# Splitting two raw weight tiles of the first two summed pairs at the FFN entry: accumulating DMA in place of two subtractions

## The chip, the cores and the metric

The kernel runs on one core of a Trainium2 chip. The metric is the device time of one execution in microseconds (us), as a median over runs. The engines are TensorE (PE in the profile; its weight loads are the row PEld), VectorE (DVE), ScalarE (ACT), GpSimd (POOL) and SyncE (SP), whose queue issues most of the DMAs. An engine name with a q behind it (SPq) is the engine's queue.

## The reference, cut to what matters

The program is one step of a two-layer streaming encoder: a Mamba-2 mixer with a SwiGLU FFN (layer 0), then banded attention with a SwiGLU FFN (layer 1), for 1024 prompt rows and 64 new rows of another stream, in float32. The change lies in the first half of the FFN, the product with `w_in`, in both layers:

```python
def swiglu(u, w_in, w_out):
    g, up = jnp.split(u @ w_in, 2, axis=-1)
    return (jax.nn.silu(g) * up) @ w_out
```

The model width is 1024. The hidden width is 2816, that is 22 tiles of 128 columns of `g` and 22 of `up`.

## The kernel before, in words

**Split operands.** Each float32 operand is split into a high part, rounded to the type float32r, and a low part, the operand less its high part. A product is three matmuls into one PSUM bank: high by high, high by low, low by high. A weight tile of 128 x 1024 comes from memory into a `raw` tile. `Weights.part` (L327) splits it into an `hl` tile with room for both parts: ScalarE copies the high part (L340), then VectorE subtracts it from the raw tile (L341). For the ring `half` (128 x 512) GpSimd does the subtraction.

**A second way to split.** Some tiles carry the mark `acc`. For them ScalarE writes the high part (L334), then its negative into the place of the low part (L335); then GpSimd issues a DMA that reads the raw weights from memory again and adds them to what stands there (L336). What is left there is the low part. Neither VectorE nor a GpSimd subtraction is used, but the low part has landed only when the DMA has. Before the change the mark is set for `w_in` tiles of the first six hidden tiles (L1256), for four of them: 0, 1, 2 and 5.

**The order of the FFN.** `ffn_plan` lists the weights in the order of their use. The first six hidden tiles are computed plainly for the first half of the rows (`plain_pairs`: one tile of `g`, one of `up`, each by eight slices of 128). While this runs, the second half of the rows is still being normalised and split (`chain`, `op_build`; L1167 to L1200 on VectorE and ScalarE). From hidden tile 6 on, the tiles of `g` and `up` are not multiplied one by one: `run_pair` forms seven products of half-size blocks in the place of eight, a Strassen-like scheme. The last six pairs of this list are the tiles 0 to 5 again, for the second half of the rows.

**A pair.** `Weights.pair` prepares a pair from its two raw tiles `r0` (of `g`) and `r1` (of `up`). With blocks b11, b21 (halves of `r0`) and b12, b22 (halves of `r1`): GpSimd computes two differences (L290, L291) into the two tiles `ta`, `tb` of the ring `tt`; `b22` is split into `half`; `r0` is split into `hl`; VectorE finishes the sums (L308, L309); `ta` and `tb` are split into `hl`. The products use them in the order r0, ta, r0, ta, tb, tb, b22. The low part of `r0` is read by the third matmul of the first product.

**Tiles that set the pace.** There are two `raw` tiles, three `hl`, two `tt` and two `half`. A raw tile is loaded anew by SP's queue (L252) when all its readers are done. An `hl` tile comes free when the last product that reads it is through: for `r0` of a pair that is the third product. So `r0` of pair 7 can be split only when TensorE is past the third product of pair 6, `ta` and `tb` of pair 7 later still. For pair 6 the seven products are run for the first half of the rows, then for the second half.

**The order on each engine.** TensorE's instructions run in the order in which the program writes them; a planner with estimated costs (`st`) fits side work between them. On the other engines a scheduler orders the instructions by readiness and priority; the copies and subtractions of `part` for the first pairs have the highest priority (`W.pri = HIP`), the accumulating DMA has none of its own. Each engine works its list in order, so an instruction that waits holds up those behind it.

**Lines that matter.** PSUM evictions of the plain tiles: L1282 (ScalarE), L1286 (VectorE). Evictions of the products: L1321 to L1341. The matmuls of the products: L1309, L1310 (high part of the weights), L1311 (low part). Splits of the second half of the rows: L1179 (ScalarE), L1180 (VectorE).

Of the kernel before, what the change touches and what calls it, by code (L numbers as in the profile page):

```python
# [12 lines left out]
ALU = mybir.AluOpType  # L13
# [20 lines left out]
FT = 22  # L34
# [29 lines left out]
NB0 = 6  # L64
# [160 lines left out]
class Weights:  # L225
# [56 lines left out]
    def pair(self, it):  # L282
        r0, r1 = it["raw"]
        b11, b21, b12, b22 = r0[:, :512], r0[:, 512:], r1[:, :512], r1[:, 512:]
        if "T" not in it:
            if not self.tt.free(2):
                return False
            ta, tb = it["T"] = self.tt.get(), self.tt.get()
            g = self.nc.gpsimd.tensor_tensor
            g(ta[:, 512:], b22, b12, op=ALU.subtract)  # L290
            g(tb[:, :512], b12, b11, op=ALU.subtract)  # L291
            return True
        ta, tb = it["T"]
        if "b22" not in it and self.half.free():
            self.part(it, "b22", self.half, b22, self.nc.gpsimd)
            it["of"][1].put()
            return True
        if "r0" not in it:
            if not self.hl.free():
                return False  # L300
            self.part(it, "r0", self.hl, r0)
            self.ready.append(it)

            return False
        if "sums" not in it:
            v = self.nc.vector.tensor_tensor
            with self.tc.high_priority(self.pri):
                v(ta[:, :512], ta[:, 512:], b11, op=ALU.add)  # L308
                v(tb[:, 512:], b21, ta[:, :512], op=ALU.subtract)  # L309
            it["of"][0].put()  # L310
            it["sums"] = True
            return True
        for key, src in (("ta", ta), ("tb", tb)):
            if key not in it:
                if not self.hl.free():
                    return False
                self.part(it, key, self.hl, src)
                self.tt.put()
                return True
        if "b22" not in it:  # L320
            return False
        self.sq.pop(0)
        return True

    def part(self, it, key, ring, v, eng=None):
        if ring is not self.half:
            ring = self.hl if ring or self.hl.free() else self.hx  # L327
            self.used.append(ring)
        t, n = ring.get(), v.shape[1]
        h, lo = t[:, 0, :n], t[:, 1, :n]  # L330
        if it.get("acc"):

            with self.tc.high_priority(self.pri):
                self.nc.scalar.copy(h, v)  # L334
                self.nc.scalar.activation(lo, h, AF.Copy, scale=-1.0)  # L335
            self.nc.gpsimd.dma_start(lo, it["src"][0], accum_op=ALU.add)  # L336
            it[key] = h, lo
            return
        with self.tc.high_priority(self.pri):
            self.nc.scalar.copy(h, v)  # L340
            (eng or self.eng or self.nc.vector).tensor_tensor(lo, v, h, op=ALU.subtract)  # L341
        it[key] = h, lo
# [32 lines left out]
def hybrid_kernel(  # L375
# [33 lines left out]
    for _ in range(17):  # L409
# [14 lines left out]
    W = Weights(  # L424
        nc, Ring(wp, "raw", RAWB, [P, 1024]), Ring(wp, "hl", HLB, [P, 2, 1024], F32R),
        Ring(None, "half", 0, [P, 2, 512], F32R), Ring(None, "tt", 0, [P, 1024]),
    )
# [826 lines left out]
    def ffn_plan(layer):  # L1254
        w1, w2 = w_f1[layer], w_f2[layer]
        W.plan(*[dict(src=[w1[i]], acc=t_ < NACC or t_ == NB0 - 1) for t_ in range(NB0) for i in (t_, FT + t_)])  # L1256
        for t_ in [*range(NB0, FT), *range(NB0)]:
            W.plan(dict(src=[w1[t_], w1[FT + t_]]))
        for s in range(NSL):
            for m in range(KD):  # L1260
                for k0, nk in KCH:
                    W.plan(dict(src=[w2[m][:, k0 * P:(k0 + nk) * P]], n=nk * P))
# [274 lines left out]
    def start_ssd(ops, px, after, dn):  # L1537
# [10 lines left out]
        st.spawn(op_build(ops[1], dn))  # L1548

    ffn_plan(0)  # L1550
    rbp = pool(ctx, "rbp", side="right")
    rba = [rbp.tile([P, 384], F32, tag=f"rbf{s}", name="rbf") for s in range(NSL)]
# [14 lines left out]
    for mg in MGS[:2] + MGS[:1] + MGS[2:] + MGS:  # L1567
        W.plan(*[dict(src=[w_o[m]]) for m in mg])
    ffn_plan(1)
    done = done2  # L1570
    uo, part_o = {}, {}
# [485 lines left out]
```

## Time and profile before

| | |
|---|---|
| median of 3 runs | 2942.54 us (2942.36 to 2943.93) |
| profiled execution, own time | 2945.22 us |
| its span in the profile | 2943.5 us |
| granted TensorE clock, mean | 0.996 |
| ScalarE splits L340 `hl` from `raw`, 128 x 1024 | 1047 ns (median) |
| VectorE subtraction L341 `hl` from `raw`, 128 x 1024 | 1224 ns (median) |
| GpSimd subtraction L341 `half` from `raw`, 128 x 512 | 1294 ns (median) |

The profile is of one execution. A row of a timeline gives the start and the length in us, engine, line, operation, and output <- input by the program's names; a bracket behind it gives the idle time of that engine before it and what released it. Matmuls overlap each other, so the distance from start to start, about 0.11 us for 256 columns, says more than the length of one. The granted clock is the share of full speed that TensorE was given.

### The profile page before, as it was taken

The numbers are of one execution on the slowest core, as the hardware profiler recorded it, in microseconds if no ns is written. First come the engines' busy times: TensorE is split into PE (matmuls) and PEld (weight loads), VectorE is DVE, ScalarE is ACT, GpSimd is POOL, SyncE is SP. The second block draws the span as 40 slices with busy tenths as digits, with TensorE's granted clock in tenths as the row PEclk, the third lists the DMA queues.
The fourth block names the chain that finished last, engine by engine and source line by source line (L and its number), as shares of the span: only waits on it lengthen the run. The fifth ranks groups of instructions, "written<-read, shape, count | busy, mean of one in ns | idle before, by whom it ended". The sixth has DMA issues, their size and how long they took to land.

```text
span 2943.5 us, 56260 instructions
## 1 busy us (share of the span) xinstructions
PE 2904.2 (99%) x21562; PEld 2864.1 (97%) x21562; DVE 2026.4 (69%) x4452; ACT 1401.6 (48%) x2531; POOL 724.4 (25%) x884
## 2 busy tenths in 40 slices
PE   8999999999999999999999999999999999999999
PEld 8999999999999999999999899999999999999999
DVE  7988878885867555583567787778688555575544
ACT  6655546454543222353445665556664322244443
POOL 1333333331022434351111000000131434351111
PEclk9999999999999999999999999999999999999999
DMA  4423333335564222345665322223376222245654
GB/s 138 132 92 106 103 100 106 100 120 159 165 187 123 76 84 73 111 151 163 206 189 157 90 80 72 64 69 103 124 204 177 79 83 73 82 153 175 223 172 137
DMA packets 202846, 368.07 MB, mean 125 GB/s; under 512 B 20688, under 2 KB 149424, under 8 KB 202576
## 3 DMA queue, kind: packets, MB, share of 16 engines
q1 hardware_dynamic: 199920, 354.97, 38.5%
q0 software_dynamic: 2656, 9.51, 1.8%
q8 instruction: 169, 2.77, 0.4%
q14 instruction: 101, 0.83, 0.1%
HBM read 297.19 MB, written 62.74 MB: 122 GB/s over the span
## 4 chain that ended last, share of the span: by engine, by line
PE 87%; DVE 6%; DMA 3%; ACT 2%; issue 1%; POOL 0%; SPq 0%; DVEq 0%; ACTq 0%; POOLq 0%
PE px L1310 9%; PE px L1311 9%; PE px L1309 9%; PE mm L463 8%; PE mm L465 8%; PE mm L464 8%; PE po L1511 6%; PE po L1512 6%; PE po L1510 6%; PE mmx L464 3%; PE mmx L465 3%; PE mmx L463 3%; PE ptp L1743 2%; PE po L1778 2%; PE S L1712 1%
## 5 line engine op out<-in xcount | busy, mean ns | idle before, releaser
L463 PE MATMUL mm<-r,hl 128*128 128x384 f32 (+2 forms) x1704 | 567.3, 333 | 2.1 <-DVE kf L1622 0.8
L465 PE MATMUL mm<-r,hl 128*128 128x384 f32 (+2 forms) x1704 | 550.7, 323 | 3.8 <-DVE hl L353 2.9
L464 PE MATMUL mm<-r,hl 128*128 128x384 f32 (+2 forms) x1704 | 549.8, 323 | 0.0
L341 DVE TENSOR_TENSOR hl<-raw,hl 128x1024 fp32r<-128x1024 f32 x216 | 254.3, 1178 | 220.1 <-ACT hl L340 218.4
L1310 PE MATMUL px<-r,hl 128*128 128x288 f32 (+1 forms) x1184 | 347.4, 293 | 0.0
L465 PEld LDWEIGHTS mm<-r,hl 128*128 128x128 f32 x1704 | 321.2, 188 | 6.0 <-DVE hl L353 4.5
L463 PEld LDWEIGHTS mm<-r,hl 128*128 128x128 f32 x1704 | 322.3, 189 | 4.3 <-DVE kf L1622 1.1
L464 PEld LDWEIGHTS mm<-r,hl 128*128 128x128 f32 x1704 | 322.3, 189 | 0.3
L1311 PE MATMUL px<-r,hl 128*128 128x288 f32 x1056 | 311.4, 295 | 0.0
L1309 PE MATMUL px<-r,hl 128*128 128x288 f32 x1056 | 310.2, 294 | 0.0
L340 ACT CAST hl<-raw 128x1024 fp32r<-128x1024 f32 x216 | 216.8, 1004 | 165.8 <-PE po L1512 103.0
L489 POOL TENSOR_TENSOR ssum<-ssum,sq 128x256 f32<-128x256 f32 (+3 forms) x97 | 124.9, 1288 | 620.0 <-ACT sq L488 604.4
L1310 PEld LDWEIGHTS px<-r,hl 128*128 128x128 f32 x1184 | 222.3, 188 | 0.0
L1311 PE MATMUL px<-rx,hl 128*128 128x256 f32 x768 | 215.0, 280 | 5.8 <-DVE hl L341 5.8
L1309 PE MATMUL px<-rx,hl 128*128 128x256 f32 x768 | 214.6, 279 | 1.8 <-DVE x L1286 1.8
L1511 PE MATMUL po<-rx,hl 128*128 128x384 f32 (+1 forms) x624 | 201.8, 323 | 0.2
L1311 PEld LDWEIGHTS px<-r,hl 128*128 128x128 f32 x1056 | 198.8, 188 | 0.0
L1309 PEld LDWEIGHTS px<-r,hl 128*128 128x128 f32 x1056 | 198.8, 188 | 0.0
L1510 PE MATMUL po<-rx,hl 128*128 128x384 f32 (+1 forms) x608 | 197.6, 325 | 0.1
L1512 PE MATMUL po<-rx,hl 128*128 128x384 f32 (+1 forms) x608 | 196.6, 323 | 0.0
L1310 PE MATMUL px<-rx,hl 128*128 128x256 f32 x640 | 179.0, 280 | 0.0
L1311 PEld LDWEIGHTS px<-rx,hl 128*128 128x128 f32 x768 | 144.9, 189 | 6.6 <-DVE hl L341 6.6
(364 smaller groups left out, 7901.7 us busy)
## 6 DMA issues: line engine op xcount, KB each, us to landing
raw<-in_w_f_dram SPq DMA_DIRECT2D x154, 512.0 KB, 3.8
rx<-in_w_f_dram SPq DMA_DIRECT2D x54, 512.0 KB, 3.6
raw<-in_w_in_dram SPq DMA_DIRECT2D x40, 512.0 KB, 3.6
MT<-ascr SPq DMA_DIRECT2D x48, 384.0 KB, 4.2
sg<-hscr SPq DMA_DIRECT2D x88, 192.0 KB, 3.5
raw<-in_w_f_dram SPq DMA_DIRECT2D x44, 384.0 KB, 3.2
raw<-in_w_so_dram SPq DMA_DIRECT2D x32, 512.0 KB, 3.7
raw<-in_w_o_dram SPq DMA_DIRECT2D x19, 512.0 KB, 3.6
```

The costliest lines, as they stand in the source:

```text
L340: self.nc.scalar.copy(h, v)
L341: (eng or self.eng or self.nc.vector).tensor_tensor(lo, v, h, op=ALU.subtract)
L463: PE.matmul(ps[:, :n], h_, xh, start=(first and i == 0), stop=False)
L464: PE.matmul(ps[:, :n], h_, xl, start=False, stop=False)
L465: PE.matmul(ps[:, :n], l_, xh, start=False, stop=(last and i == nk - 1))
L489: (eng or G).tensor_tensor(ssum[:, :n], ssum[:, :n], q[:, :n], op=ALU.add)
L1309: PE.matmul(ps, wh, ah[:, k, :], start=(k == 0), stop=False)
L1310: PE.matmul(ps, wh, al[:, k, :], start=False, stop=False)
L1311: PE.matmul(ps, wl, ah[:, k, :], start=False, stop=(k == 3))
L1510: PE.matmul(ps[:, :n], wh, xh, start=(k == 0), stop=False)
L1511: PE.matmul(ps[:, :n], wh, xl, start=False, stop=False)
L1512: PE.matmul(ps[:, :n], wl, xh, start=False, stop=(k == FT - 1))
```

## The change

For the summed pairs 6 and 7 of each layer (the first two, `NB0` and `NB0 + 1`), the low part of the raw tile `r0` and the low part of the block `b22` are made in the second way: ScalarE writes the high part and its negative, and a DMA issued by GpSimd adds the raw weights from memory, 512 KB for `r0` and 256 KB for `b22`. The sums `ta` and `tb` are split as before, and so are all other pairs. The list of weights for the second half of the rows is walked in the order 6 to 21, then 0 to 5; the new mark `pacc` is set only for 6 and 7.

```diff
@@ pair(self, it)
-            self.part(it, "b22", self.half, b22, self.nc.gpsimd)
+            self.part(it, "b22", self.half, b22, self.nc.gpsimd, it["pacc"] and it["src"][1][:, 512:])
...
-            self.part(it, "r0", self.hl, r0)
+            self.part(it, "r0", self.hl, r0, None, it["pacc"] and it["src"][0])
@@ part
-    def part(self, it, key, ring, v, eng=None):
+    def part(self, it, key, ring, v, eng=None, acc=None):
...
         if it.get("acc"):
+            acc = it["src"][0]
+        if acc is not None and acc is not False:
 
             with self.tc.high_priority(self.pri):
                 self.nc.scalar.copy(h, v)
                 self.nc.scalar.activation(lo, h, AF.Copy, scale=-1.0)
-            self.nc.gpsimd.dma_start(lo, it["src"][0], accum_op=ALU.add)
+            self.nc.gpsimd.dma_start(lo, acc, accum_op=ALU.add)
             it[key] = h, lo
             return
@@ ffn_plan
-            W.plan(dict(src=[w1[t_], w1[FT + t_]]))
+            W.plan(dict(src=[w1[t_], w1[FT + t_]], pacc=t_ in (NB0, NB0 + 1)))
```

## The prediction

> **What bounds the kernel now.** First the page: the span beside TensorE's busy time.
>
> ```profile
> span 2943.5 us, 56260 instructions
> ...
> PE 2904.2 (99%) x21562; PEld 2864.1 (97%) x21562; DVE 2026.4 (69%) x4452; ACT 1401.6 (48%) x2531; POOL 724.4 (25%) x884
> ```
>
> TensorE is busy for 2904.2 of 2943.5 us, so only what stops or slows its stream moves the end. The change touches the two FFN entries (layer 0 near 917 us, layer 1 near 2263 us), so next comes TensorE's timeline there, only the rows with idle time before them. The bracket is that idle time and what released it.
>
> ```profile
> 918.84 0.38 PE L1311 MATMUL px<-rx,hl 128*128 128x256 f32 x1 [0.47 <-DVE hl L341]
> ...
> 924.80 0.36 PE L1309 MATMUL px<-rx,hl 128*128 128x256 f32 x1 [1.82 <-DVE x L1286]
> ...
> 927.11 0.58 PE L1311 MATMUL px<-rx,hl 128*128 128x256 f32 x1 [1.83 <-DVE hl L341]
> ```
> ```profile
> 2266.29 0.39 PE L1311 MATMUL px<-rx,hl 128*128 128x256 f32 x1 [1.94 <-DVE hl L341]
> ...
> 2272.21 0.38 PE L1311 MATMUL px<-rx,hl 128*128 128x256 f32 x1 [1.56 <-DVE hl L341]
> ...
> 2275.73 0.38 PE L1309 MATMUL px<-rx,half 128*128 128x256 f32 x1 [0.74 <-DVE p L1326]
> ```
>
> Layer 0 loses 0.47 + 1.82 + 1.83 = 4.12 us and layer 1 1.94 + 1.56 + 0.74 = 4.24 us, every time to VectorE: to the low parts of `ta` and `tb` of pair 6 (L341), or to an eviction that stands behind other VectorE work. Third view, the table of windows (length; busy time of PE, PEld, DVE, ACT, POOL; granted clock; DMA share; GB/s), for what the stops do to the clock:
>
> ```profile
> 926.00:928.00 2.00, 0.89 (x4) 0.90 (x5) 2.00 (x3) 0.00 (x0) 0.87 (x1) 0.77 0.00 0
> 928.00:930.00 2.00, 2.00 (x11) 2.00 (x11) 1.90 (x4) 0.42 (x1) 0.41 (x1) 0.50 0.31 61
> 930.00:932.00 2.00, 2.00 (x18) 2.00 (x17) 0.91 (x3) 0.04 (x1) 0.00 (x0) 0.88 0.57 209
> ```
> ```profile
> 2264.00:2266.00 2.00, 0.35 (x3) 0.15 (x2) 2.00 (x2) 2.00 (x3) 1.15 (x1) 1.00 0.02 4
> ```
>
> After its two long stops, with two matmuls between them, layer 0 runs at a granted clock of 0.50 for a while. The clock missing is 2 x (0.23 + 0.50 + 0.12) = 1.7 us. Layer 1 has a stop of 1.94 us and keeps 1.00. So at most 4.12 + 1.7 + 4.24 = 10.1 us can be won at the entries.
>
> **Part 1: what goes at the entries.** For pairs 6 and 7 VectorE loses the 128x1024 subtraction of `r0` and GpSimd the 128x512 subtraction of `b22`. Layer 0, VectorE then GpSimd, ScalarE and SP's queue:
>
> ```profile
> 911.36 1.21 DVE L341 TENSOR_TENSOR hl<-raw,hl 128x1024 fp32r<-128x1024 f32 x1
> ...
> 919.04 2.12 DVE L1180 TENSOR_TENSOR r<-r 128x1152 fp32r<-128x1152 f32 x1
> 922.36 0.69 DVE L308 TENSOR_TENSOR tt<-tt,raw 128x512 f32<-128x512 f32 x1 [1.19 <-POOL tt L290]
> 922.97 1.35 DVE L1180 TENSOR_TENSOR r<-r 128x1152 fp32r<-128x1152 f32 x1
> ...
> 925.84 1.22 DVE L341 TENSOR_TENSOR hl<-tt,hl 128x1024 fp32r<-128x1024 f32 x1
> ```
> ```profile
> 909.15 1.74 POOL L341 TENSOR_TENSOR half<-raw,half 128x512 fp32r<-128x512 f32 x1
> 917.77 2.18 POOL L341 TENSOR_TENSOR half<-raw,half 128x512 fp32r<-128x512 f32 x1 [6.88 <-ACT half L340]
> 919.89 2.43 POOL L290 TENSOR_TENSOR tt<-raw 128x512 f32<-128x512 f32 x1
> ```
> ```profile
> 917.07 0.62 ACT L340 CAST half<-raw 128x512 fp32r<-128x512 f32 x1 [0.76 <-DMA raw<-in_w_f_dram]
> ```
> ```profile
> 912.60 0.33 SPq L252 DMA_DIRECT2D raw<-in_w_f_dram  x1
> ```
>
> The last stop of layer 0 ends when `tb`'s low part is done (VectorE, 925.84). Back from there, VectorE waits 1.19 us at L308 for GpSimd's L290, which stood behind the `b22` subtraction (917.77, 2.18 us). With that subtraction gone, L290 starts when `ta`'s tile is free, and the 1.19 goes. L290 also lay beside L1180, which took 2.12 us there and 1.35 in the next row; apart, 0.77 more goes. The removed `r0` subtraction (911.36, 1.21) would add to this, but the 919.04 step waits for its ScalarE cast, queued behind the `b22` cast, and that waits for a weight load (917.07). The load is issued at 912.60 as the raw tile comes free, so it goes out some 1 us earlier, but it meets the new transfers, and ScalarE has one more `b22` pass (about 0.6). I take this as no gain. Layer 0: 1.19 + 0.77 = 2.0 us. Some 2.1 us of stops is left, about layer 1's 1.94 that kept the clock, so the 1.7 us of slow clock goes too: 3.7 us. From below 0 (ScalarE's extra passes delay the same casts), from above 4.1 + 1.7 = 5.8.
>
> Here the Trainium skill speaks. "TensorE: Matmul & The Clock Gate", section "Why this matters for your kernels", asks for no idle gap over about 3 us if the clock is to hold. Layer 0's gaps of 1.82 and 1.83 us lost it nonetheless; read strictly, the rule gives nothing for fewer stops, and the sum below would be 1.7 us worse. I go by the rows.
>
> Layer 1, VectorE and then GpSimd and ScalarE:
>
> ```profile
> 2256.63 1.21 DVE L341 TENSOR_TENSOR hl<-raw,hl 128x1024 fp32r<-128x1024 f32 x1
> ...
> 2263.94 2.29 DVE L341 TENSOR_TENSOR hl<-tt,hl 128x1024 fp32r<-128x1024 f32 x1
> ...
> 2270.95 1.21 DVE L341 TENSOR_TENSOR hl<-tt,hl 128x1024 fp32r<-128x1024 f32 x1
> ```
> ```profile
> 2262.65 2.50 POOL L341 TENSOR_TENSOR half<-raw,half 128x512 fp32r<-128x512 f32 x1 [7.19 <-ACT half L340]
> ```
> ```profile
> 2261.95 0.62 ACT L340 CAST half<-raw 128x512 fp32r<-128x512 f32 x1 [7.01 <-DMA raw<-in_w_f_dram]
> ```
>
> `ta`'s low part takes 2.29 us beside GpSimd's `b22` subtraction (2262.65) and 1.21 alone (2270.95): 1.08 us goes. The `r0` subtraction (1.21) stands ahead of it in an unbroken VectorE stretch: together 2.3. `ta`'s cast, too, stands behind the waiting `b22` cast and its extra 0.6, with the load behind it some 1 us earlier. I take 2.1 us, between 0 and 4.24.
>
> **Part 2: what is added, pair 6.** ScalarE gets `-h` passes, GpSimd DMA issues; the tiles ahead of the pairs that already go this way show both. The first two rows are the view of a source line (min/median/max ns), the third its landings after issue, then landings of the two issues ahead of each entry (DMA view of a window, its median; layer 0, layer 1), and the one of the kernel's first issue of this kind:
>
> ```profile
> L335 ACT ACTIVATE hl<-hl x13: 1043/1053/1066, 59.9 to 2247.4; 128x1024 fp32r<-128x1024 f32 x13
> ```
> ```profile
> L336 POOL DMA_DIRECT2D hl<-in_w_f_dram x11: 844/859/872, 837.6 to 2248.8; - x11
> ...
> DMA to landing us min/median/max: 5.4/8.0/10.5
> ```
> ```profile
> hl<-in_w_f_dram POOLq DMA_DIRECT2D x2, 512.0 KB, 7.5
> ```
> ```profile
> hl<-in_w_f_dram POOLq DMA_DIRECT2D x2, 512.0 KB, 6.3
> ```
> ```profile
> hl<-in_w_in_dram POOLq DMA_DIRECT2D x1, 512.0 KB, 5.4
> ```
>
> On GpSimd the `b22` issue (0.86) takes the place of the subtraction at 909.15, and the issue for `r0` of pair 6 follows it: issued near 910.0, landed at 915.4 to 920.5. The low part's first use in layer 0:
>
> ```profile
> 916.85 0.28 PE L1311 MATMUL px<-rx,hl 128*128 128x256 f32 x1
> ```
>
> So a new stop of 0 to 3.7 us can stand there. It costs nothing as long as it is shorter than the stop still left at `tb` (2.1 us): both are waits up to a fixed moment. I take 0; uncovered, up to 3.7 - 2.1 = 1.6 us, and the same in layer 1. `b22` is read last of seven products: 0, covered by six products.
>
> **Part 3: pair 7, the price.** Its `r0` gets a tile only when TensorE has done with pair 6's `r0`. The ScalarE cast that starts then, and the first matmul that reads the low part, in layers 0 and 1:
>
> ```profile
> 937.62 1.05 ACT L340 CAST hl<-raw 128x1024 fp32r<-128x1024 f32 x1 [2.78 <-PE px L1311]
> ```
> ```profile
> 944.00 0.28 PE L1311 MATMUL px<-rx,hl 128*128 128x256 f32 x1
> ```
> ```profile
> 2282.17 1.05 ACT L340 CAST hl<-raw 128x1024 fp32r<-128x1024 f32 x1 [1.83 <-PE px L1311]
> ```
> ```profile
> 2288.55 0.28 PE L1311 MATMUL px<-rx,hl 128*128 128x256 f32 x1
> ```
>
> Both ends hang on TensorE and move together, so the distance stays: 6.38 us in each layer. The subtraction fitted into it. The new way takes two ScalarE passes (2 x 1.05, with some 0.05 between them: 2.15 us) and the landing, so it is late by landing + 2.15 - 6.38 = landing - 4.23. With the entries' own landings: 7.5 - 4.23 = 3.3 us in layer 0, 6.3 - 4.23 = 2.1 us in layer 1, together 5.4. From below 5.4 gives 1.2 per layer, from above 10.5 gives 6.3. I take the nearest rows. Behind the waiting GpSimd issue stands pair 8's L290, which waits for its own load anyway:
>
> ```profile
> 943.73 2.16 POOL L290 TENSOR_TENSOR tt<-raw 128x512 f32<-128x512 f32 x1 [9.57 <-DMA raw<-in_w_f_dram]
> ```
>
> `b22` of pair 7 is again covered.
>
> A rule speaks against the change: "SBUF — State Buffer", section "SBUF: two separate sides", says that a DMA from GpSimd's queue cannot get its descriptors written while certain VectorE instructions hold the port that the two share. The 11 issues above took 844 to 872 ns, so none was held, but the landings do spread; the rule's result would be the first rival.
>
> **Sum.** -3.7 - 2.1 + 5.4 = -0.4 us. The profiled execution took 2945.22 us with its span of 2943.5, so it would take 2944.8; the median of the three runs is 2942.54, which becomes 2942.1.
>
> **The rivals.** (1) Slower: pair 7's landing is late. A landing of 9.0 gives 4.8 us per layer, one gap long enough to lose the clock as 3.65 us of stops did in layer 0 (1.7 each): 2 x 6.5 - 5.8 = +7.2, 2949.7. The point from which it decides is 5.8 + 5.9 = 11.7 us for both, 5.85 each less 1.7, a landing of 8.4. For it: 8.0 is the median of all; against it: the four issues nearest to the entries landed in 7.5 and 6.3. (2) The entry gain doesn't come, because ScalarE's extra passes and the added transfers delay the casts: +5.4 less at most 1 = about +4.9, 2947.4. For it: 917.07 and 2261.95 both wait for loads. (3) The entries lose nearly all their stops and landings are 5.4: -10.1 + 2.4 = -7.7, 2934.8. Against it: the load waits, and 5.4 is the landing of the kernel's first issue, far from the entries.
>
> **How the numbers follow.** Forecast, gains and the new stops about equal: 0.55, own range 2938 to 2946. Rival 1 0.20, rival 2 0.18, rival 3 0.07. A measurement of this kernel can tell about 0.2% (5.9 us) from no change. Faster takes rival 3: 0.07. Slower takes rival 1 and a sixth of rival 2: 0.23. The same: 0.70. The range, 2936 to 2950, leaves out the outer halves of rivals 1 and 3.
>
> **What would show it.** Right: L308 near 922 without its GpSimd wait, clock 1.00 through 932, and a new stop of 2 to 3 us before the third matmul of pair 7, released by a DMA to `hl`. Wrong: no such stop, a landing above 8.4, a clock of 0.50 near 945, or stops at `ta` and `tb` as long as before.

## The result, and the profile after

The changed kernel takes 2952.36 us (median of 5 runs, 2949.39 to 2957.22) against 2942.36 us before (5 runs, 2939.75 to 2943.93) on the same chip: a ratio of 1.0037, interval [1.0027, 1.0048]. It is slower by about 10 us where 2942.1 us was forecast. On another chip a repeat gave 2951.75 against 2943.64 us (28 runs of the kernel before), 1.0031 [1.0020, 1.0043]. The profiled execution is one of the quicker ones, 2950.64 us with a span of 2948.9 (2945.22 and 2943.5 before); its times must not be taken for the median.

In the changed kernel the lines behind the edit have moved by two: L336, L337, L338 are the new way's copy, negative and transfer, L342 and L343 the old copy and subtraction, L1311 and L1313 the matmuls. First the top of the page:

```profile
span 2948.9 us, 56282 instructions
...
PE 2904.3 (98%) x21562; PEld 2863.6 (97%) x21562; DVE 2019.5 (68%) x4448; ACT 1407.9 (48%) x2539; POOL 723.7 (25%) x888
```

TensorE's busy time is the same (2904.2 before), VectorE is busy 6.9 us less, and the span is 5.4 us longer. So TensorE stands still more. Its timeline, only rows with idle time, first layer 0, then layer 1:

```profile
918.06 0.38 PE L1313 MATMUL px<-rx,hl 128*128 128x256 f32 x1 [1.68 <-DMA hl<-in_w_f_dram]
924.26 0.35 PE L1311 MATMUL px<-rx,hl 128*128 128x256 f32 x1 [0.69 <-DVE x L1288]
926.56 0.39 PE L1313 MATMUL px<-rx,hl 128*128 128x256 f32 x1 [1.83 <-DVE hl L343]
945.56 0.38 PE L1313 MATMUL px<-rx,hl 128*128 128x256 f32 x1 [1.88 <-DMA hl<-in_w_f_dram]
```
```profile
2264.28 0.39 PE L1313 MATMUL px<-rx,hl 128*128 128x256 f32 x1 [1.19 <-DMA hl<-in_w_f_dram]
2266.98 0.39 PE L1311 MATMUL px<-rx,hl 128*128 128x256 f32 x1 [1.25 <-ACT hl L342]
2268.24 0.38 PE L1313 MATMUL px<-rx,hl 128*128 128x256 f32 x1 [0.75 <-DVE hl L343]
2275.39 0.38 PE L1313 MATMUL px<-rx,hl 128*128 128x256 f32 x1 [1.16 <-DVE hl L343]
2293.78 0.39 PE L1313 MATMUL px<-rx,hl 128*128 128x256 f32 x1 [2.78 <-DMA hl<-in_w_f_dram]
```

Two things are to be seen. The entries have not become better: 1.68 + 0.69 + 1.83 = 4.20 us in layer 0 (4.12 before) and 1.19 + 1.25 + 0.75 + 1.16 = 4.35 us in layer 1 (4.24 before). And each layer has a new stop at pair 7 (945.56 and 2293.78), 1.88 + 2.78 = 4.66 us, released by the new transfer. The table of windows for layer 1 (eighth number: granted clock) shows a third thing:

```profile
2268.00:2270.00 2.00, 1.76 (x10) 1.76 (x11) 1.79 (x3) 2.00 (x3) 1.73 (x1) 0.70 0.71 119
2270.00:2272.00 2.00, 2.00 (x11) 2.00 (x10) 1.36 (x2) 2.00 (x4) 0.60 (x1) 0.50 0.20 66
2272.00:2274.00 2.00, 2.00 (x19) 2.00 (x17) 2.00 (x3) 1.42 (x3) 0.00 (x0) 0.94 0.10 32
```

Layer 1's entry, which kept its clock before, now loses it once: 2 x (0.30 + 0.50 + 0.06) = 1.7 us. Layer 0's entry loses it as before. Stops and clock make 0.08 + 0.11 + 4.66 + 1.7 = 6.6 us, against 5.4 us between the two profiled spans. Clock is also lost far from the change, now here and now there: by the windows over the whole span 8.5 us in the execution before and 5.1 in the changed one. With that the sum is 3.2 us, so some 2 us between these two executions are in no stop and no lost clock.

Why the entries gained nothing is read from what stood ahead of the casts. SP's queue and ScalarE in layer 0, then ScalarE in layer 1:

```profile
909.76 0.33 SPq L252 DMA_DIRECT2D raw<-in_w_f_dram  x1
```
```profile
918.83 0.63 ACT L336 CAST half<-raw 128x512 fp32r<-128x512 f32 x1 [5.45 <-DMA raw<-in_w_f_dram]
```
```profile
2264.44 0.62 ACT L336 CAST half<-raw 128x512 fp32r<-128x512 f32 x1 [9.32 <-DMA raw<-in_w_f_dram]
```

The load of pair 7's second raw tile goes out at 909.76 (912.60 before), but the cast that needs it starts at 918.83 (917.07 before). The DMA view of the half microsecond in which that load is issued, first in the kernel before, then in the changed one (size, and us from issue to landing):

```profile
raw<-in_w_f_dram SPq DMA_DIRECT2D x1, 512.0 KB, 4.4
```
```profile
hl<-in_w_f_dram POOLq DMA_DIRECT2D x1, 512.0 KB, 9.3
raw<-in_w_f_dram SPq DMA_DIRECT2D x1, 512.0 KB, 9.1
```

The load takes 9.1 us in place of 4.4 (in layer 1 8.5 in place of 4.1), beside the accumulating transfer for pair 6's `r0`, which takes 9.3. "DMA: Bandwidth & Descriptors" of the Trainium skill, section "Issuing engines are not separate DMA queues", says that transfers interleave on the same engines whichever engine has issued them; these rows agree, SP's load being slowed by GpSimd's.

### The profile page after: what moved, and what is told of

It reads as the page before. It is cut to its first block, busy times and chain, and to the rows that moved or that the text cites. A ratio compares the mean times of both kernels' runs of the same rounds, so it can differ in the third digit from the quotient of the medians.

```text
span 2948.9 us, 56282 instructions
## 1 busy us (share of the span) xinstructions
PE 2904.3 (98%) x21562; PEld 2863.6 (97%) x21562; DVE 2019.5 (68%) x4448; ACT 1407.9 (48%) x2539; POOL 723.7 (25%) x888
## 4 chain that ended last, share of the span: by engine, by line
PE 86%; DVE 6%; DMA 3%; ACT 2%; issue 2%; POOL 0%; SPq 0%; DVEq 0%; ACTq 0%; POOLq 0%
PE px L1313 9%; PE px L1312 9%; PE px L1311 9%; PE mm L465 8%; PE mm L467 7%; PE mm L466 7%; PE po L1513 6%; PE po L1514 6%; PE po L1512 6%; PE mmx L466 3%; PE mmx L467 3%; PE mmx L465 3%; PE ptp L1745 2%; PE po L1780 2%; PE S L1714 1%
## 5 line engine op out<-in xcount | busy, mean ns | idle before, releaser
L343 DVE TENSOR_TENSOR hl<-raw,hl 128x1024 fp32r<-128x1024 f32 x212 | 248.7, 1174 | 219.7 <-ACT hl L342 216.4
L1313 PE MATMUL px<-r,hl 128*128 128x288 f32 x1056 | 311.4, 295 | 0.0
L1311 PE MATMUL px<-r,hl 128*128 128x288 f32 x1056 | 310.3, 294 | 0.0
L342 ACT CAST hl<-raw 128x1024 fp32r<-128x1024 f32 x212 | 212.7, 1003 | 161.9 <-PE po L1514 102.6
L1313 PE MATMUL px<-rx,hl 128*128 128x256 f32 x768 | 216.1, 281 | 11.3 <-DMA hl<-in_w_f_dram 7.5
L1311 PE MATMUL px<-rx,hl 128*128 128x256 f32 x768 | 215.4, 281 | 1.9 <-ACT hl L342 1.3
L1311 PEld LDWEIGHTS px<-r,hl 128*128 128x128 f32 x1056 | 198.7, 188 | 0.1
L1313 PEld LDWEIGHTS px<-r,hl 128*128 128x128 f32 x1056 | 198.8, 188 | 0.0
L1313 PEld LDWEIGHTS px<-rx,hl 128*128 128x128 f32 x768 | 145.7, 190 | 12.7 <-DMA hl<-in_w_f_dram 8.3
```

The costliest lines, as they stand in the source:

```text
L1311: PE.matmul(ps, wh, ah[:, k, :], start=(k == 0), stop=False)
L1313: PE.matmul(ps, wl, ah[:, k, :], start=False, stop=(k == 3))
```

## The experiments

**Theory A**, formed from these rows: `r0` of pair 6 slows the load for pair 7, which ScalarE's `b22` cast waits for, and the casts behind it set the entry; `r0` of pair 7 lands too late; both stops can cost clock besides. **Rival B**: it is the extra ScalarE passes and GpSimd issues, not the bytes. **Rival C**: it is all pair 7. Each kernel was compared with the kernel before on the same chip.

| kernel | us | before | ratio | 95% interval |
|---|---|---|---|---|
| e1 the change again | 2951.75 | 2943.64 | 1.0031 | 1.0020 to 1.0043 |
| e2 pair 6 alone | 2947.20 | 2943.64 | 1.0011 | 1.0002 to 1.0021 |
| e3 pair 7 alone | 2948.05 | 2943.64 | 1.0019 | 1.0010 to 1.0028 |
| e4 short transfers | 2937.93 | 2943.64 | 0.9981 | 0.9972 to 0.9990 |
| e5 `b22` in both pairs | 2938.93 | 2943.80 | 0.9981 | 0.9972 to 0.9990 |
| e6 `b22` in pair 7 | 2941.00 | 2943.80 | 0.9993 | 0.9984 to 1.0002 |
| e7 transfers nobody needs | 2946.27 | 2943.80 | 1.0009 | 1.0001 to 1.0018 |
| e8 `b22` at low priority | 2942.67 | 2943.80 | 1.0000 | 0.9992 to 1.0009 |
| e9 copies out | 2945.68 | 2943.78 | 1.0006 | 0.9997 to 1.0015 |
| e10 `r0` in both pairs | 2951.86 | 2943.78 | 1.0031 | 1.0020 to 1.0042 |
| e11 `b22`, and `r0` by GpSimd | 2940.04 | 2943.78 | 0.9991 | 0.9982 to 1.0001 |
| e12 `b22` in both, `r0` of pair 6 | 2945.15 | 2944.47 | 1.0006 | 0.9997 to 1.0015 |

**e1, the changed kernel once more.** No edit.

> The changed kernel once more, for a second profile and its spread. Theory A (the extra transfers at the entry delay the weight load for pair 7's b22, so the entry gain is lost, and pair 7's first product waits for its landing): the same, 2949 to 2957 us, with the two stops of pair 7 (1.9 and 2.8 us in the first profile) and a load that lands after about 9 us at both entries. If the spread comes from the clock, this profile shows 0.50 in other windows than the first.

Its time came as expected. At the entries its profile has stops of 2.98 us in layer 0 (4.20 in the first profile) and 4.58 in layer 1, at pair 7 one of 1.74 us (layer 0) and the following in layer 1. Its clock was lost near 920 us, again near 2268 us, and near 2295 us; in the first profile it was lost near 929 us and near 2270 us.

```profile
2293.04 0.38 PE L1313 MATMUL px<-rx,hl 128*128 128x256 f32 x1 [3.45 <-DMA hl<-in_w_f_dram]
```

The same stop is thus 2.78 us in one execution and 3.45 in another, and the clock goes with it or not.

**e2 and e3, one pair alone.**

```diff
-            W.plan(dict(src=[w1[t_], w1[FT + t_]], pacc=t_ in (NB0, NB0 + 1)))
+            W.plan(dict(src=[w1[t_], w1[FT + t_]], pacc=t_ == NB0))        # e2
+            W.plan(dict(src=[w1[t_], w1[FT + t_]], pacc=t_ == NB0 + 1))    # e3
```

> The mark is set for pair 6 alone. Theory A: pair 7's two stops go (4.7 us, and any clock lost there), the entries stay as bad as with the change: 2944 to 2947 us. Rival B (the loss lies at the entries, through ScalarE's extra passes for pair 6 and GpSimd's issues): 2950 us or more. Rival C (all of the loss is pair 7): 2941 us or less.

> The mark is set for pair 7 alone. Theory A: the stops of pair 7 stay (4.7 us), but no extra transfer runs while pair 7's raw tiles are loaded, so those land after 4 to 5 us as before, and GpSimd's b22 subtraction of pair 7 is off VectorE's path (2 us in layer 0, 1 in layer 1): 2943 to 2947 us. Rival B: as before the change or faster, 2942 us or less. Rival C: 2950 us or more.

Pair 6 alone costs 3.6 us (0.2 us over A's range), pair 7 alone 4.4 us (a microsecond over A's range), and the two add up to 8.0 us, against 8.1 for the whole change on the same chip (e1). Neither half holds it all, so C falls, and so does B as it was stated for these two runs. In e3 the stops at pair 7 were 2.04 and 3.97 us, and the clock was lost at both of them. The first, and the windows around it:

```profile
942.74 0.39 PE L1313 MATMUL px<-rx,hl 128*128 128x256 f32 x1 [2.04 <-DMA hl<-in_w_f_dram]
```
```profile
942.00:944.00 2.00, 1.26 (x11) 1.26 (x11) 2.00 (x3) 0.00 (x0) 2.00 (x2) 1.00 0.24 76
944.00:946.00 2.00, 2.00 (x11) 2.00 (x10) 0.47 (x1) 0.37 (x1) 2.00 (x2) 0.51 0.04 8
946.00:948.00 2.00, 2.00 (x13) 2.00 (x12) 0.00 (x0) 0.40 (x1) 0.36 (x1) 0.64 0.56 170
```

One stop of 2.04 us took the clock to 0.50 for some 3 us: 2 x (0.49 + 0.36) = 1.7 us more, almost as much as the stop itself.

**e4, the same instructions with short transfers.**

```diff
-            self.nc.gpsimd.dma_start(lo, acc, accum_op=ALU.add)
+            m = n if it.get("acc") else n // 8
+            self.nc.gpsimd.dma_start(lo[:, :m], acc[:, :m], accum_op=ALU.add)
```

> The changed kernel, but each new accumulating transfer moves an eighth of its columns (128 of 1024, 64 of 512); the low part of the other columns stays the negative high part, so the product leaves the low part's sum out there. All instructions and issues stay. Theory A: the weight load of pair 7 lands after 4 to 5 us again, both entries win about 2 us each, the landing of pair 7's low part falls to 3 us or so and its stops go: 2935 to 2940 us. Rival B: entries as slow as with the change; only pair 7's stops go, about 2947 us.

This is the cleanest cut between A and B: every ScalarE pass and every GpSimd issue stays, and the kernel is 5.7 us faster than before. Only 1.49 us of stops are left in layer 0 and 0.31 + 0.70 + 1.84 us in layer 1, none at pair 7. So the bytes of the transfers do it, and B falls. In layer 0 the load takes longer than A said (4 to 5 us): 5.5, beside a landing of 6.1 us for a mere 64 KB. At pair 7 of layer 0 such a transfer landed after 2.8 us, as A said.

```profile
raw<-in_w_f_dram SPq DMA_DIRECT2D x1, 512.0 KB, 5.5
hl<-in_w_f_dram POOLq DMA_DIRECT2D x1, 64.0 KB, 6.1
```

**e5 and e6, only b22.** The `r0` line is put back; e6 also sets the mark for pair 7 alone.

```diff
-            self.part(it, "r0", self.hl, r0, None, it["pacc"] and it["src"][0])
+            self.part(it, "r0", self.hl, r0)
```

> Only b22 takes the new way, in pairs 6 and 7; both r0 are subtracted by VectorE as before. Theory A: no stop at pair 7, a third of the extra bytes at the entry, GpSimd's subtractions gone: the weight load lands after 5 to 6 us and each entry wins 0 to 2 us: 2939 to 2943 us. Rival B (ScalarE's extra passes and GpSimd's issues cost the entry): 2944 us or more.

> Only b22 of pair 7 takes the new way. Theory A: nothing is added while pair 7's raw tiles load (4 to 5 us), L290 of pair 7 no longer waits for a subtraction: the stops of each entry fall by about 1 us, as with the mark on pair 7 alone, and pair 7 has no stop: 2940 to 2943 us. Rival B: 2944 us or more.

`b22` in both pairs is faster than both kernels: 4.9 us less than before, 0.9981 [0.9972, 0.9990], just under A's range. e6 lies in A's range, but its interval touches no change. The stops of e5, TensorE's timeline in layer 0 and layer 1, and the cast behind the load (issued at 906.95):

```profile
918.09 0.36 PE L1311 MATMUL px<-rx,hl 128*128 128x256 f32 x1 [0.64 <-DVE x L1288]
920.40 0.39 PE L1313 MATMUL px<-rx,hl 128*128 128x256 f32 x1 [1.84 <-DVE hl L343]
```
```profile
2260.06 0.39 PE L1313 MATMUL px<-rx,hl 128*128 128x256 f32 x1 [1.80 <-DVE hl L343]
```
```profile
912.16 0.62 ACT L336 CAST half<-raw 128x512 fp32r<-128x512 f32 x1 [1.55 <-DMA raw<-in_w_f_dram]
```

2.48 us are left in layer 0 and 1.80 in layer 1, 4.1 us less than before, and the load takes about 5.2 us. That is the size of the entry gain that the prediction worked out for the whole change (2.0 + 2.1 us of stops), got without `r0`; the 1.2 us that `r0`'s subtraction was to give in layer 1 came another way, which these rows don't separate.

**e7, transfers that nobody needs.** Put behind the split of pair 6's `r0`, in the kernel before:

```diff
+            if it["dead"]:
+                d = self.dead.pop(0)
+                self.nc.gpsimd.dma_start(d[:, :512], it["src"][1][:, 512:])
+                self.nc.gpsimd.dma_start(d[:, 512:], it["src"][0])
```

> The kernel before with two more GpSimd transfers behind the split of pair 6's r0, which read the same 256 and 512 KB of weights and write them to memory that nobody reads. Nothing waits for them. Theory A: the load of pair 7's second raw tile lands after 7 to 9 us in place of 4.5, the ScalarE cast of b22 starts 2 to 4 us later, and each entry loses 1 to 4 us: 2946 to 2951 us. Rival B: the load may land later but the time stays within 2 us of before.

The time lies in A's range and says nothing for A. Since the transfers depend on nothing, the scheduler put them at the start of the program. The view of their line:

```profile
L304 POOL DMA_DIRECT2D dead<-in_w_f_dram x2: 533/546/559, 3.3 to 4.4; - x2
```

They were issued at 3.3 to 4.4 us and ran beside the kernel's first weight loads, three of which took 8.3 us to land (median) in place of 4.8. So plain copies from memory to memory, 1.5 MB of them, slow loads too, but nothing was added at the entries: the experiment failed, and its time without its trace would have misled. e9 gives the transfers a source that ties them to the entry.

**e9, copies of what the casts leave.** The same, with the sources `it["b22"][0]` and `it["r0"][0]`, so that the transfers start when the casts are done.

> The kernel before with two more GpSimd transfers that can only start when pair 6's b22 and r0 are cast, since they copy those high parts (256 and 512 KB) to memory that nobody reads. Nothing else waits for them. Theory A (transfers beside the load of pair 7's second raw tile are enough to do the harm): that load lands after 6 to 9 us in place of 4.4, the ScalarE cast of b22 starts 1.5 to 4 us later, the stops of each entry grow by 1 to 4 us: 2946 to 2951 us. Rival B (ScalarE's extra passes do it): stops as before, 2944 us.

The load (issued at 909.34) landed after this time:

```profile
raw<-in_w_f_dram SPq DMA_DIRECT2D x1, 512.0 KB, 6.1
```

That is 1.7 us more than before from transfers alone. But the stops grew only to 4.42 and 4.26 us, and 1.0006 [0.9997, 1.0015] can't be told from no change; A's range is missed. So transfers beside the load do slow it, as A says, but these plain copies, which go from the tiles to memory, slow it by a third of what the accumulating ones do (4.7 us), and don't reproduce the harm. Plain transfers of the same bytes from memory into tiles were not tested at the entry.

**e8, no transfer added, b22 split at ordinary priority.**

```diff
+            p, self.pri = self.pri, 0
             self.part(it, "b22", self.half, b22, self.nc.gpsimd)
+            self.pri = p
```

> The kernel before, with the split of b22 of the first pair(s) at ordinary priority in place of the highest, so that the scheduler can put pair 6's ta and tb casts ahead of the wait for pair 7's weights. No transfer is added. Theory A, by which ScalarE's queue behind that wait sets the entry: the stops of each entry fall by 1 to 2 us: 2938 to 2942 us. If the order on ScalarE and GpSimd doesn't change: 2943 us.

Nothing gained: 1.0000. In layer 1 the order stayed, the `b22` cast still waiting 7.07 us for its load ahead of `ta`'s cast; so the order on ScalarE was not tested there. In layer 0 one cast of the rows (L1181) moved ahead of it.

**e10, only r0; e11, r0 of pair 6 by GpSimd; e12, no r0 of pair 7.**

```diff
+            self.part(it, "b22", self.half, b22, self.nc.gpsimd)                           # e10
+            self.part(it, "r0", self.hl, r0, it["first"] and self.nc.gpsimd)               # e11
+            self.part(it, "r0", self.hl, r0, None, it["first"] and it["src"][0])           # e12
```

Here `first` is true for pair 6 alone.

> Only r0 takes the new way, in pairs 6 and 7; b22 is subtracted by GpSimd as before. Theory A: pair 7's two stops stay (4.7 us), two thirds of the extra bytes stay at the entry, and GpSimd's b22 subtraction stays ahead of L290: 2949 to 2954 us, not faster than the whole change. If the harm were in b22's part: 2945 us or less.

> b22 of pairs 6 and 7 the new way, r0 of pair 6 subtracted by GpSimd, which then has nothing else between L291 and L290 of pair 7. VectorE loses 1.2 us ahead of ta and no transfer of 512 KB is added. Theory A: if VectorE's queue ahead of tb still sets the last stop, 0.5 to 1.5 us per entry less than with b22 alone: 2936 to 2939 us; if GpSimd's read beside VectorE's splits slows these by as much, the same as b22 alone, 2939 us.

> The whole change less r0 of pair 7, which VectorE subtracts as before; so it is b22 in both pairs (2938.9 us) and r0 of pair 6. Theory A: pair 7's stops go, but the 512 KB for r0 of pair 6 still delay the load of pair 7's second raw tile to 8 or 9 us, so the entries stop as long as with the whole change (4.2 and 4.4 us): 2944 to 2948 us, 5 to 9 more than with b22 alone. If r0 of pair 6 were harmless: 2939 us.

e10 is as slow as the whole change (1.0031 both), without any of `b22`'s transfers: `r0` is the harm. Its loads at the entries took 7.5 and 7.1 us, its pair 7 stops were 1.90 and 1.79 us. e12 shows what is left when pair 7's `r0` goes back to VectorE: no stop at pair 7, the load still 8.7 us (8.1 in layer 1), stops of 2.02 + 0.39 + 1.84 = 4.25 and 0.94 + 1.28 + 0.76 + 1.19 = 4.17 us, as long as with the change, and 1.0006, as A expected. e5 lies 0.0025 below e12, or 7 us, e12 as much below the change: about half of `r0`'s harm is pair 6's load, half pair 7's stop. e11 adds no byte to `b22`'s 256 KB beside the load, but 2.85 us of GpSimd's work in layer 0 (2.70 in layer 1), and the load goes out 6.0 us after GpSimd's first difference (L290) where in e5 it was 5.2. It isn't faster than e5, and lies 1 us above the range that A gave for a gain. The load of e12 in layer 0, beside pair 6's `r0`:

```profile
hl<-in_w_f_dram POOLq DMA_DIRECT2D x1, 512.0 KB, 9.1
raw<-in_w_f_dram SPq DMA_DIRECT2D x1, 512.0 KB, 8.7
```

## Why the prediction was wrong, point by point

**What bounds the kernel** held: every difference found is a stop of TensorE or its clock, at the entries or at pair 7 (e7 apart).

**Part 1, the entry gain, failed**, and in one step: "The load is issued at 912.60 as the raw tile comes free, so it goes out some 1 us earlier, but it meets the new transfers, and ScalarE has one more `b22` pass (about 0.6). I take this as no gain." That put what the transfers do to the load at about nothing; it was 4.7 us. The load went out 2.8 us earlier but took 9.1 us in place of 4.4, so the cast behind it came later, not at the same time. The waits of VectorE that were to go did go (before pair 7's L308, at 921.82, no wait for GpSimd is left in layer 0); in their place VectorE waited 4.30 us for ScalarE:

```profile
920.55 1.36 DVE L1182 TENSOR_TENSOR r<-r 128x1152 fp32r<-128x1152 f32 x1 [4.30 <-ACT r L1181]
```

The 3.7 + 2.1 = 5.8 us came out as -0.2, and with the clock lost in layer 1 as about -1.9. That such a gain was there to be had is shown by e4 and e5, where the load takes 5.5 and 5.2 us: 5.7 and 4.9 us faster. This is the mechanism of the second rival, with the transfers rather than the passes as its cause. That rival was priced without lost clocks, and the first rival, which had them, with the full entry gain; both came together, and the time lies above the range.

**The clock** was half right. The prediction took 1.7 us for one loss, and that is what each loss measured. But it counted on a stop of about 2 us to leave the clock alone, since one of 1.94 had done so; in e3 one of 2.04 did not, in e10 not one of 1.79 at pair 7 of layer 1. The rule that it weighed, in the Trainium skill's "TensorE: Matmul & The Clock Gate", section "Why this matters for your kernels" (no gap over about 3 us), would have let all of these pass; the measurement decides against it here. What also counts is where in time a stop lies. In every trace here a slow stretch lasts 3.41 us or twice that (the last one, at the program's end, apart), and within one trace two of them begin a whole number of 3.41 us apart: in e3 at 923.55 and 944.03, that is 6 x 3.41. So a trace can be laid out in slots of 3.41 us. The slot of e3 that holds the whole stop of 2.04 us, and the next; then the two slots of the changed kernel over which its stop of 2.78 us is spread (third number: TensorE busy; eighth: granted clock):

```profile
940.62:944.03 3.41, 1.37 (x12) 1.29 (x12) 3.41 (x4) 0.51 (x1) 3.41 (x3) 1.00 0.50 114
944.03:947.44 3.41, 3.41 (x17) 3.41 (x16) 0.44 (x1) 0.66 (x2) 2.33 (x2) 0.50 0.23 55
```
```profile
2289.30:2292.71 3.41, 1.70 (x14) 1.49 (x12) 1.61 (x3) 1.99 (x3) 2.25 (x3) 1.00 0.85 167
2292.71:2296.12 3.41, 2.34 (x18) 2.34 (x19) 3.41 (x4) 0.37 (x1) 2.25 (x2) 1.00 0.17 49
```

The shorter stop fills 2.04 us of one slot, and the next slot runs at 0.50; the longer one leaves 1.71 and 1.07 us idle in two slots, and the clock holds. In the 14 traces 27 of the 28 slots with 2.0 us or more of idle TensorE are followed by a slow one (the other is the first of a program), and of the 55 slots with 1.5 to 2.0 us of it 17 are, so no sharp limit shows. The stop of 1.94 us on which the prediction rested lay across two slots, 0.76 and 1.18 us: that it kept the clock was luck. The same page of the Trainium skill, section "What's actually happening", says that the window over which activity is judged runs freely. These traces agree.

**Part 2, pair 6.** "issued near 910.0, landed at 915.4 to 920.5" held: issued at 908.74, landed at 918.05. Its stops (1.68 and 1.19 us) were not what set the entry: `tb`'s low part came last, as predicted. What this transfer did to others was not priced at all beyond "meets the new transfers".

**Part 3, pair 7,** was right in mechanism and nearly in size: 3.3 + 2.1 = 5.4 us forecast, 1.88 + 2.78 = 4.66 us measured. That the sums lie so near is in part luck, since each layer was off by 0.7 to 1.4 us, in opposite directions. From cast to issue it took 2.64 us, not 2.15, because an eviction stands between the passes on ScalarE and GpSimd's issue starts 0.3 us after the second; the landings were 5.8 and 6.6 us, not 7.5 and 6.3. GpSimd's two issues took 0.89 and 0.88 us, against 0.84 to 0.87 for those of the kernel before, so none was held up. Layer 0:

```profile
937.13 1.05 ACT L336 CAST hl<-raw 128x1024 fp32r<-128x1024 f32 x1 [2.77 <-PE px L1313]
938.09 0.44 ACT L1329 ACTIVATE p<-p 128x288 f32<-128x288 f32 x1
938.43 1.04 ACT L337 ACTIVATE hl<-hl 128x1024 fp32r<-128x1024 f32 x1
```
```profile
939.77 0.89 POOL L338 DMA_DIRECT2D hl<-in_w_f_dram  x1 [6.09 <-ACT hl L337]
```

The clock that such stops can cost was left to the first rival; e1 and e3 lost it there, the first profile did not.

**The sum.** -5.8 + 5.4 became about +0.2 + 4.7 of stops, and one to two lost clocks more. In the profiled execution that is 6.6 us. For the executions without a kept trace the recorded mean clock of each run (to 0.001, or 2.9 us) gives the share. Time by (1 - clock), as a mean over the runs, is 11.8 us in e1 (6 runs) and 8.1 us in the kernel before on the same chip (28 runs). So of the 8.4 us between their mean times some 3.7 are clock, and the other 4.7 fit the stops (+0.2 + 4.7). It stays open why accumulating transfers slow a load three times as much as plain copies out of the same tiles.

## What to carry to other kernels

A transfer that spares an engine a subtraction is not free because nothing waits for it at once: ask which loads run beside it, and who stands in line behind the first instruction that waits for those. Move the small and late operand (here `b22`, read last of seven) that way, and leave the one that is read first to an engine. Where a tile becomes free only when the next use is near, compare that distance (6.4 us here) with the whole way from cast to landing (8.4 to 9.2 us), not with the work saved.

## What the runs showed of the hardware that was not expected

An accumulating transfer of 512 KB slowed a load of 512 KB beside it from between 4.1 and 4.4 us to 7.5 and 7.1 (e10), with 256 KB more of the kind to between 8.1 and 9.3, plain copies of 768 KB out of tiles only to 6.1 and 5.4. Beside loads the landing of an accumulating transfer falls far less than its size: at the entry of layer 0 9.3 us for 512 KB and still 6.1 for 64 KB. Single stops of TensorE of 1.8 to 2.1 us took the granted clock to 0.50 for 3.41 us, 1.7 us lost each time, in some executions and not in others. Slow stretches keep to slots of 3.41 us: with 2.0 us or more of idle TensorE in one slot the next was slow (27 of 28), while a stop of 2.78 us across two slots cost no clock.
